# A two-layer encoder with streamed weights: one 512-column matmul in place of two of 256 in the weights-stationary products

## The chip, the cores and the metric

The kernel runs on one core of a Trainium2 chip. The metric is the device time of one execution in microseconds (us). The engines of the core work beside one another, each through its own list of instructions in a fixed order: TensorE (PE) multiplies matrices into PSUM, VectorE (DVE) and ScalarE (ACT) do elementwise work, GpSimd (POOL) does a little of it too, and SyncE (SP) issues most DMA transfers. An instruction waits at the head of its engine's list until the data and the buffers that it needs are there.

## The reference

The reference is an encoder trunk of two layers on 256 tokens of width 2048, all in float32. Cut to what is computed:

```python
for l in range(2):
    h = rmsnorm(x, attn_norm[l])
    qd, kd, vd, qn, kn, vn = split(h @ w_in[l])          # six blocks of 1024 columns
    o_diff = diff_attention(rope(qd), rope(kd), vd)      # 8 heads: softmax1 - lam * softmax2, then rmsnorm
    o_na   = rmsnorm(neighbourhood_attention(qn, kn, vn, rpb[l]))   # 8 heads, windows on a 4 x 64 grid
    x = x + concat(o_diff, o_na) @ w_out[l]
    u = relu(rmsnorm(x, mlp_norm[l]) @ w_mlp_in[l])      # 2048 -> 8192
    x = x + (u * u) @ w_mlp_out[l]                       # 8192 -> 2048
return rmsnorm(x, final_norm)
```

## The kernel before

**Numbers in two halves.** Every operand of a large product is split into a high half, rounded to the format that TensorE takes at full rate (fp32r), and a low half, what the rounding left. A product a·w is then three matmuls: a_hi·w_hi, a_lo·w_hi and a_hi·w_lo. Activations lie transposed in `hT` tiles, 16 of them (one for each 128 of the 2048 input columns), each with 256 high columns and, next to them in the same tile, 256 low columns.

**The weight stream.** The weights come in 384 slabs of 128 x 2048 float32 (1 MB). `next_slab` loads one into a `raw` buffer (three of them), ACT copies each half of 1024 columns to `whi` (line 130) and DVE subtracts to get `wlo` (line 131); there are four buffers of each.

**Two kinds of product.** `block_product` streams the weights through TensorE: 512 columns of weights move past 128 x 128 blocks of activations (lines 153 to 155), for two tiles of 128 tokens. `stationary_product` does it the other way round: a 128 x 128 block of weights is loaded into TensorE and the 256 tokens move past it, 16 blocks after one another into one PSUM tile `accu` of 128 x 256, three matmuls of 256 columns each (lines 180 to 182). It serves the queries and keys of the neighbourhood-attention heads (two products for each of 8 heads, in each of two layers, 32 in all) and the first product of the MLP (64 for each layer, 128 in all): 160 products of 16 steps, 2560 steps.

**What takes the results.** `accu` shares four PSUM banks with the `acc` tiles of `block_product` (tag "acc"). Queries go through `split_plain` (lines 276, 277), keys are first multiplied by `rb` (line 376); in the MLP ACT takes the Relu (`rl`, line 524) and DVE multiplies it by `accu` (line 526, u2), and `split` makes halves of that (lines 136, 137).

**The attention heads.** A differential head transposes its weights `wd` (line 296), ACT copies them out of PSUM (`wT`, line 303), PE multiplies by v (line 307), ACT squares the result with a running sum (`junk`, line 365), POOL makes a scale of it (lines 189, 191, 369), DVE applies it (`o`, line 315), PE transposes (line 318) and ACT and DVE split it into `mix` (lines 136, 137). A neighbourhood head transposes its weights `pr` (line 296), ACT and DVE split them (`half`, lines 276, 277), and PE multiplies by `vs` (lines 410 to 412). These PSUM results are called `tp` and share two banks. In SBUF, tag "o" is a ring of four buffers, in which a new tile waits until the one four before it is no longer read; `o`, `rl`, `u2` and a few smaller tiles are in it.

**The order.** The instructions of each engine are put in order at build time by the framework's scheduler, which simulates the program. So a change in the duration or number of instructions moves others too: PE's list mixes the long products with the small matmuls of the heads, and what stands between a small matmul and the next that needs its result is time in which ACT, DVE and POOL do their part.

Of the kernel before, what the change touches and what calls it, by code (L numbers as in the profile page):

```python
# [18 lines left out]
P = 128  # L19
# [16 lines left out]
NB = 512  # L36
NEG = -1.0e30
RUN = 5 * RPB_C + GRID_W
# Where a query of column 0 and an even row finds its last neighbour in a head's reversed table.
RPB_FIRST = RPB_HEAD - 1 - (10 * RPB_C + GRID_W - 1 + WIN_C - 1)  # L40
N_CHUNK = 4
F_PER_CHUNK = D_FF // P // N_CHUNK
SLABS = 48 + 16 + 64 + 64
# Column blocks of 512 of the input projection: q, k, v of the differential heads 0-3, then 4-7.
DIFF_BLOCKS = [0, 2, 4, 1, 3, 5]
NA_Q, NA_K, NA_V = 3 * HALF, 4 * HALF, 5 * HALF

# [1 line left out]
def body(ctx, tc, x, x_t, w, gains_in, gains_o, final_g, lam_in, rpb, ident_in, rope_in, mask_in, out):  # L49
# [5 lines left out]
    small = ctx.enter_context(tc.tile_pool(name="small", bufs=4))  # L55
    ps = ctx.enter_context(tc.tile_pool(name="ps", bufs=2, space=PSUM))

# [1 line left out]
    gin = const.tile([P, 2 * DEPTH, NK], F32, name="gin")  # L59
    nc.scalar.dma_start(gin, gains_in)  # L60
    ident = const.tile([P, P], F32, name="ident")
# [3 lines left out]
    xs = [const.tile([P, D], F32, name=f"x{t}") for t in range(NT)]  # L65

    def stream(dst, src):
        """A load on the queue of the weights, in the order of the program."""
        tc.keep_in_program_order(nc.sync.dma_start(dst, src))

    lam_sb = [None]

    def load_table(l):
        """The relative position biases of a layer, from where each query reads its windows."""
        table = act.tile([P, HEADS, RUN + 1], F32, name="table", tag="table", bufs=1)
        for rr in range(P // GRID_W):
            src = bass.AP(tensor=rpb.tensor,
                          offset=rpb.offset + l * HEADS * RPB_HEAD + RPB_FIRST + rr * RPB_C,
                          ap=[[1, GRID_W], [RPB_HEAD, HEADS], [1, RUN]])
            stream(table[rr * GRID_W:(rr + 1) * GRID_W, :, :RUN], src)  # L80
        return table
# [23 lines left out]
    ones = const.tile([P, P], F32, name="ones")  # L105
    nc.vector.memset(ones, 1.0)

# [1 line left out]
    slab_no = [0]  # L109
    x_rest = [None]  # L110

# [26 lines left out]
                                       op0=ALU.mult, op1=ALU.subtract)  # L138

    def block_product(n_k, operand, before=None, split_tail=0):  # L140
        """[256, 512] = sum over n_k blocks of 128 of operand(k)^T @ the next slabs. The last
        `split_tail` slabs are held together, so that one tile of tokens ends before the other."""
        acc = [ps.tile([P, NB], F32, name="acc", tag="acc", bufs=4) for _ in range(NT)]
        parts = []
        todo = []

        def one(k, t):
            hi, lo = parts[k // 2]
            c0 = (k % 2) * NB
            a = operand(k)  # L150
            wh, wl = hi[:, c0:c0 + NB], lo[:, c0:c0 + NB]
            ah, al = a[:, 0, t * P:(t + 1) * P], a[:, 1, t * P:(t + 1) * P]
            nc.tensor.matmul(acc[t], ah, wh, start=k == 0, stop=False)  # L153
            nc.tensor.matmul(acc[t], al, wh, start=False, stop=False)  # L154
            nc.tensor.matmul(acc[t], ah, wl, start=False, stop=k == n_k - 1)  # L155

        n_s = n_k // 4
        for s in range(n_s):
            if before is not None:
                before(s)  # L160
            parts += next_slab()
            todo += range(4 * s, 4 * s + 4)
            if s < n_s - split_tail:
                for k in todo:
                    for t in range(NT):
                        one(k, t)
                todo = []
        for t in range(NT):
            for k in todo:
                one(k, t)  # L170
        return acc

    def stationary_product(h_t):
        """[128, 256] = the next slab^T @ normed activations, transposed."""
        parts = next_slab()
        acc = ps.tile([P, S], F32, name="accu", tag="acc", bufs=4)
        for k in range(NK):
            hi, lo = parts[k // 8]
            wh, wl = hi[:, (k % 8) * P:(k % 8 + 1) * P], lo[:, (k % 8) * P:(k % 8 + 1) * P]
            nc.tensor.matmul(acc, wh, h_t[k][:, 0], start=k == 0, stop=False)  # L180
            nc.tensor.matmul(acc, wh, h_t[k][:, 1], start=False, stop=False)  # L181
            nc.tensor.matmul(acc, wl, h_t[k][:, 0], start=False, stop=k == NK - 1)  # L182
        return acc

# [1 line left out]
    def rms_scale(ss, n, width):  # L186
        """(ss / width + EPS) ** -0.5 on [128, n]."""
        v = small.tile([P, n], F32, name="v")
        nc.gpsimd.tensor_scalar(v, ss, 1.0 / width, EPS, op0=ALU.mult, op1=ALU.add)
        r = small.tile([P, n], F32, name="r")  # L190
        nc.gpsimd.tensor_tensor(r, v, mhalf[:, :n], op=ALU.pow)
        return r

    class Norm:
        """RMSNorm of x in pieces: the gain goes into the transposed halves, the scale of
        each token comes out of `scale()` and is applied to the products."""

        def __init__(self, gain):
            self.gain = gain
# [12 lines left out]
            self.h_t[k] = h  # L212

        def take(self, n):
            """Columns n*512... of x are final."""
            for t in range(NT):
                self.squares(n, t)
            for k in range(4 * n, 4 * n + 4):
                pt = ps.tile([P, S], F32, name="tp", tag="tp", bufs=2)
                for t in range(NT):  # L220
                    nc.tensor.transpose(pt[:, t * P:(t + 1) * P], xs[t][:, k * P:(k + 1) * P], ident)  # L221
                self.store(k, pt)
# [5 lines left out]
                self._r[t] = rms_scale(tot, 1, D)  # L228
            return self._r[t]

# [1 line left out]
    def to_sbuf_rope(acc, r, which):  # L232
        """Rotary position of q (which 0) or k (which 1), then transposed: [(m d), head, token]."""
        dst = [act.tile([P, 4, S], F32R, name="qkT", tag="A", bufs=12) for _ in range(2)]
        for t in range(NT):
            nat = work.tile([P, NB], F32, name="nat", tag="nat", bufs=3)
# [41 lines left out]
        return hi, lo  # L278

    def along_free(r):  # L280
        """[128, 256]: r of every token, in all partitions."""
        pb = ps.tile([P, S], F32, name="tp", tag="tp", bufs=2)
        for t in range(NT):
            diag = work.tile([P, P], F32, name="diag", tag="o", bufs=4)
            nc.vector.tensor_scalar(diag, ident, r[t], None, op0=ALU.mult)
            nc.tensor.matmul(pb[:, t * P:(t + 1) * P], ones, diag, start=True, stop=True)
        rb = work.tile([P, S], F32, name="rb", tag="rb", bufs=1)
        nc.scalar.activation(rb, pb, AF.Copy)
        return rb

    def transposed_weights(pr):
        """[128 queries, tile, 256 keys] -> [128 keys, tile, 256 queries] in PSUM."""
        pw = ps.tile([P, NT, S], F32, name="tp", tag="tp", bufs=2)
        for t in range(NT):
            for kt in range(NT):
                nc.tensor.transpose(pw[:, kt, t * P:(t + 1) * P], pr[:, t, kt * P:(kt + 1) * P], ident)  # L296
        return pw

    def weights_times_v(pr, v, j):
        """pr [128 q, tile, 256 keys] -> [128 q, tile, 128] in PSUM."""  # L300
        pw = transposed_weights(pr)
        wt = work.tile([P, NT, S], F32, name="wT", tag="wT", bufs=3)
        nc.scalar.activation(wt, pw, AF.Copy)
# [5 lines left out]
        return po  # L309

    def to_mix(po, scale, gain):
        """Scaled rows of po, transposed, with the gain, split."""
        o = work.tile([P, NT, HD], F32, name="o", tag="o", bufs=4)
        for t in range(NT):
            nc.vector.tensor_scalar(o[:, t, :], po[:, t, :], scale[:, t:t + 1], None, op0=ALU.mult)
        pt = ps.tile([P, S], F32, name="tp", tag="tp", bufs=2)
        for t in range(NT):
            nc.tensor.transpose(pt[:, t * P:(t + 1) * P], o[:, t, :], ident)
        return split_mix(pt, gain)
# [106 lines left out]
            else:  # L426
                nc.vector.scalar_tensor_tensor(sl, acc[t], scale[t], sl, op0=ALU.mult, op1=ALU.add)

# [1 line left out]
    norm = Norm(0)  # L430

    def prologue(s):
        """The transposed x comes in beside the first slabs, x itself and the tables behind them."""
        st = act.tile([P, 4, S], F32, name="xT", tag="A", bufs=12)

        def load(k0, k1):
# [10 lines left out]
    for l in range(DEPTH):  # L447
        if l == 0:
            first = [block_product(NK, norm.h_t.__getitem__, before=b) for b in (prologue, load_constants)]
            for t in range(NT):  # L450
                for n in range(4):
                    norm.squares(n, t)
            # lambda, and the sub-norm's gain times 1 - lambda_init
            lq = lam_sb[0].rearrange("p l (a b) d -> p l a b d", b=2)
            prod = work.tile([P, DEPTH, 2, QKD], F32, name="prod", tag="o", bufs=4)
            for i in range(DEPTH):
# [62 lines left out]
        for c in range(N_CHUNK):  # L519
            us = []  # L520
            for f in range(F_PER_CHUNK):
                acc = stationary_product(h_t)
                rl = work.tile([P, S], F32, name="rl", tag="o", bufs=4)
                nc.scalar.activation(rl, acc, AF.Relu)
                u2 = work.tile([P, S], F32, name="u2", tag="o", bufs=4)
                nc.vector.tensor_mul(u2, acc, rl)
                if f % 2 == 0:
                    pair = act.tile([P, 2, 2, S], F32R, name="u2T", tag="A", bufs=12)
                split(pair[:, f % 2, 0], pair[:, f % 2, 1], u2, 1.0)
# [13 lines left out]
                        nxt.take(n)  # L543
        norm = nxt

# [1 line left out]
    for t in range(NT):  # L547
        r = norm.scale(t)
        for n in (3, 0, 1, 2):
# [27 lines left out]
def _pack_weights(w_in, w_out, w_mlp_in, w_mlp_out):  # L577
    slabs = np.empty((DEPTH, SLABS, P, 2048), np.float32)

    def moving(a):  # L580
        """[K, N] -> [N / 512, K / 512, 128, 4 * 512]"""
        K, N = a.shape
        a = a.reshape(K // NB, 4, P, N // NB, NB).transpose(3, 0, 2, 1, 4)
        return a.reshape(N // NB, K // NB, P, 2048)

    def stationary(a):
        """[2048, N] -> [N / 128, 128, 16 * 128]"""
        return a.reshape(NK, P, -1, P).transpose(2, 1, 0, 3).reshape(-1, P, 2048)

    for l in range(DEPTH):  # L590
# [54 lines left out]
```

## Time and profile before

| | before |
|---|---|
| median of 3 runs | 2261.7 us (2261.6 to 2261.77) |
| span of the profiled execution | 2259.7 us |
| PE busy | 2244.5 us, 99% |
| DVE busy | 1296.5 us, 57% |
| ACT busy | 1063.4 us, 47% |
| POOL busy | 91.9 us, 4% |

The profiler took one execution. The whole of that execution was not timed apart from its span; the median of the runs is 2.0 us above the span, and that much is taken to lie around it. The shares are those of the span. "PE busy" counts an engine with work in its pipeline; how fast the pipeline goes is read from the distance of one matmul's start to the next one's.

### The profile page before, as it was taken

What the parts mean: (1) busy time and instruction counts of PE and PEld (TensorE: products, weight loads), DVE (VectorE), ACT (ScalarE), POOL (GpSimd) and SP (SyncE); (2) the same over time, 40 slices, a digit from 0 to 9 for tenths busy, and PEclk for the clock granted to TensorE, in tenths of its full rate; (3) what the DMA queues carried; (4) which work ended last, traced back from release to release, by engine and by line L of the source; (5) the groups of instructions that cost most, each with busy time, mean ns of one, the idle gap of its engine ahead of it and who ended that gap; (6) DMA issues with size and microseconds to landing.
All of it is one profiled execution on the core that took longest, in us unless ns stands there. A gap on an engine that the chain in (4) does not pass through costs nothing.

```text
span 2259.7 us, 33741 instructions
## 1 busy us (share of the span) xinstructions
PE 2244.5 (99%) x13904; PEld 2019.3 (89%) x13904; DVE 1296.5 (57%) x1615; ACT 1063.4 (47%) x1579; POOL 91.9 (4%) x136
## 2 busy tenths in 40 slices
PE   8999999999999999999999999999999999999998
PEld 7889998998998898899888899989989989988986
DVE  6656666655555555555566666665555555555554
ACT  6556454543444444344445564545434434444443
POOL 1111000000000000000010110000000000000000
PEclk9999999999999999999999999999999999999999
DMA  9453445555555545555654434455555555455553
GB/s 326 149 186 135 173 161 186 184 179 196 187 187 186 190 183 189 198 178 185 202 188 162 168 140 170 179 191 180 187 188 186 186 193 192 179 197 189 186 188 131
DMA packets 61306, 414.63 MB, mean 183 GB/s; under 512 B 7008, under 2 KB 9184, under 8 KB 11872
## 3 DMA queue, kind: packets, MB, share of 16 engines
q1 hardware_dynamic: 60720, 411.40, 50.8%
q8 instruction: 109, 1.79, 0.3%
q10 hardware_dynamic: 432, 1.08, 0.2%
q14 instruction: 45, 0.37, 0.0%
HBM read 410.35 MB, written 2.10 MB: 183 GB/s over the span
## 4 chain that ended last, share of the span: by engine, by line
PE 99%; DMA 0%; DVE 0%; ACT 0%; SPq 0%; issue 0%; POOL 0%; ACTq 0%; POOLq 0%
PE acc L155 18%; PE acc L153 18%; PE acc L154 18%; PE accu L180 14%; PE accu L182 14%; PE accu L181 14%; PE tp L307 1%; PE tp L296 1%; PE tp L221 0%; PE sc L343 0%; DMA raw<-in_w 0%; PE tp L257 0%; PE sc L345 0%; PE sc L344 0%; PE tp L412 0%; PE sc L387 0%
## 5 line engine op out<-in xcount | busy, mean ns | idle before, releaser
L131 DVE TENSOR_TENSOR wlo<-raw,whi 128x1024 fp32r<-128x1024 f32 (+1 forms) x770 | 945.7, 1229 | 848.0 <-ACT whi L130 841.4
L130 ACT ACTIVATE whi<-raw 128x1024 fp32r<-128x1024 f32 (+1 forms) x770 | 814.7, 1059 | 1055.5 <-PE acc L154 548.9
L181 PE MATMUL accu<-hT,whi 128*128 128x256 f32 x2560 | 726.0, 284 | 0.0
L182 PE MATMUL accu<-hT,wlo 128*128 128x256 f32 x2560 | 724.6, 283 | 0.0
L180 PE MATMUL accu<-hT,whi 128*128 128x256 f32 x2560 | 724.0, 283 | 0.0
L181 PEld LDWEIGHTS accu<-hT,whi 128*128 128x128 f32 x2560 | 491.5, 192 | 0.5
L180 PEld LDWEIGHTS accu<-hT,whi 128*128 128x128 f32 x2560 | 490.8, 192 | 0.8
L182 PEld LDWEIGHTS accu<-hT,wlo 128*128 128x128 f32 x2560 | 491.4, 192 | 0.0
L154 PE MATMUL acc<-whi,u2T 128*128 128x512 f32 x1024 | 399.2, 390 | 0.0
L153 PE MATMUL acc<-whi,u2T 128*128 128x512 f32 x1024 | 398.7, 389 | 0.0
L155 PE MATMUL acc<-wlo,u2T 128*128 128x512 f32 x1024 | 398.5, 389 | 0.0
L155 PEld LDWEIGHTS acc<-wlo,u2T 128*128 128x128 f32 x1024 | 192.3, 188 | 39.7
L153 PEld LDWEIGHTS acc<-whi,u2T 128*128 128x128 f32 x1024 | 192.3, 188 | 39.6
L154 PEld LDWEIGHTS acc<-whi,u2T 128*128 128x128 f32 x1024 | 192.3, 188 | 39.3
L153 PE MATMUL acc<-whi,hT 128*128 128x512 f32 x512 | 202.7, 396 | 6.0 <-ACT whi L130 6.0
L154 PE MATMUL acc<-whi,hT 128*128 128x512 f32 x512 | 203.0, 397 | 0.0
L155 PE MATMUL acc<-wlo,hT 128*128 128x512 f32 x512 | 199.4, 395 | 0.1
L153 PEld LDWEIGHTS acc<-whi,hT 128*128 128x128 f32 x512 | 96.9, 189 | 26.3 <-ACT whi L130 6.2
L155 PEld LDWEIGHTS acc<-wlo,hT 128*128 128x128 f32 x512 | 96.7, 189 | 20.3 <-DVE wlo L131 0.5
L154 PEld LDWEIGHTS acc<-whi,hT 128*128 128x128 f32 x512 | 96.9, 189 | 19.7
L154 PE MATMUL acc<-whi,mix 128*128 128x512 f32 x256 | 100.7, 393 | 0.0
L153 PE MATMUL acc<-whi,mix 128*128 128x512 f32 x256 | 100.7, 393 | 0.0
(117 smaller groups left out, 1331.9 us busy)
## 6 DMA issues: line engine op xcount, KB each, us to landing
raw<-in_w SPq DMA_DIRECT2D x383, 1024.0 KB, 4.8
x<-in_x SPq DMA_DIRECT2D x2, 1024.0 KB, 9.7
out<-xg SPq DMA_DIRECT2D x8, 256.0 KB, 3.1
table<-in_rpb SPq DMA_DIRECT2D x4, 438.0 KB, 11.5
xT<-in_x_t SPq DMA_DIRECT2D x3, 512.0 KB, 9.5
raw<-in_w SPq DMA_DIRECT2D x4, 256.0 KB, 5.4
gb<-in_final_g ACTq DMA_DIRECT2D x2, 512.0 KB, 5.7
xT<-in_x_t SPq DMA_DIRECT2D x2, 256.0 KB, 3.5
```

What stands on the lines that cost most here:

```text
L130: nc.scalar.activation(hi[:, c:c + step], r, AF.Copy)
L131: nc.vector.tensor_sub(lo[:, c:c + step], r, hi[:, c:c + step].bitcast(F32))
L153: nc.tensor.matmul(acc[t], ah, wh, start=k == 0, stop=False)
L154: nc.tensor.matmul(acc[t], al, wh, start=False, stop=False)
L155: nc.tensor.matmul(acc[t], ah, wl, start=False, stop=k == n_k - 1)
L180: nc.tensor.matmul(acc, wh, h_t[k][:, 0], start=k == 0, stop=False)
L181: nc.tensor.matmul(acc, wh, h_t[k][:, 1], start=False, stop=False)
L182: nc.tensor.matmul(acc, wl, h_t[k][:, 0], start=False, stop=k == NK - 1)
L296: nc.tensor.transpose(pw[:, kt, t * P:(t + 1) * P], pr[:, t, kt * P:(kt + 1) * P], ident)
L307: nc.tensor.matmul(po[:, t, :], wt[:, kt, t * P:(t + 1) * P], v[:, kt, j * HD:(j + 1) * HD], start=kt == 0, stop=kt == NT - 1)
```

## The change

`stationary_product` now issues two matmuls for each of its 16 steps instead of three. The first has 512 columns: the high and the low halves of the activations move past one load of the high weights, and their products go to the two halves of a PSUM tile that is now 512 columns wide. The second multiplies the low weights by the high activations and adds to the first half, as before. After the last step ACT copies the second half of the tile to SBUF (`low`, line 184) and DVE adds it to the first half (`whole`, line 186). What the function returns is therefore in SBUF, in the ring with tag "o". In the MLP the Relu on ACT goes, and DVE makes relu(u)·u in one instruction. Line numbers behind line 186 grow by four (line 296 becomes 300, 307 becomes 311, 318 becomes 322, 410 to 412 become 414 to 416). Comments are taken out, and the program gets a constant for a DMA scratch size.

```diff
     def stationary_product(h_t):
         parts = next_slab()
-        acc = ps.tile([P, S], F32, name="accu", tag="acc", bufs=4)
+        acc = ps.tile([P, NB], F32, name="accu", tag="acc", bufs=4)
         for k in range(NK):
             hi, lo = parts[k // 8]
             wh, wl = hi[:, (k % 8) * P:(k % 8 + 1) * P], lo[:, (k % 8) * P:(k % 8 + 1) * P]
-            nc.tensor.matmul(acc, wh, h_t[k][:, 0], start=k == 0, stop=False)
-            nc.tensor.matmul(acc, wh, h_t[k][:, 1], start=False, stop=False)
-            nc.tensor.matmul(acc, wl, h_t[k][:, 0], start=False, stop=k == NK - 1)
-        return acc
+            nc.tensor.matmul(acc, wh, h_t[k].rearrange("p a b -> p (a b)"), start=k == 0, stop=False)
+            nc.tensor.matmul(acc[:, :S], wl, h_t[k][:, 0], start=False, stop=k == NK - 1)
+        low = work.tile([P, S], F32, name="low", tag="low", bufs=2)
+        nc.scalar.activation(low, acc[:, S:], AF.Copy)
+        whole = work.tile([P, S], F32, name="whole", tag="o", bufs=4)
+        nc.vector.tensor_add(whole, acc[:, :S], low)
+        return whole
...
                 acc = stationary_product(h_t)
-                rl = work.tile([P, S], F32, name="rl", tag="o", bufs=4)
-                nc.scalar.activation(rl, acc, AF.Relu)
                 u2 = work.tile([P, S], F32, name="u2", tag="o", bufs=4)
-                nc.vector.tensor_mul(u2, acc, rl)
+                nc.vector.scalar_tensor_tensor(u2, acc, 0.0, acc, op0=ALU.max, op1=ALU.mult)
...
-    nc = bacc.Bacc("TRN2", target_bir_lowering=False, num_devices=1)
+    nc = bacc.Bacc("TRN2", target_bir_lowering=False, num_devices=1, dynamic_dma_scratch_size=4096)
```

The scheduler's order changes with it. Two places are shown. The first, **place A**, is the end of the differential heads, where the products of the neighbourhood heads begin. On PE before, in the first layer: `tp_1534` and `tp_1596` are the transposes of two heads' results `o`, `tp_1570` and `tp_1633` those of two heads' weights `wd`, `tp_1577` a head's product with v, and `accu_...` are weights-stationary products:

```order
L318 MATMUL tp_1534<-ident_75,o_1531 128x128
L181 MATMUL accu_1882<-hT_202,whi_1878 128x256
L318 MATMUL tp_1534<-ident_75,o_1531 128x128
L296 MATMUL tp_1570<-ident_75,wd_1567 128x128 x4
...
L307 MATMUL tp_1577<-v_1411,wT_1575 128x128 x4
...
L318 MATMUL tp_1596<-ident_75,o_1593 128x128
...
L296 MATMUL tp_1633<-ident_75,wd_1630 128x128 x4
```

The same place on PE now, with nothing left out:

```order
L182 MATMUL accu_1870<-hT_256,wlo_1867 128x256
L322 MATMUL tp_1534<-ident_75,o_1531 128x128 x2
L300 MATMUL tp_1570<-ident_75,wd_1567 128x128 x4
L311 MATMUL tp_1577<-v_1411,wT_1575 128x128 x4
L322 MATMUL tp_1596<-ident_75,o_1593 128x128 x2
L300 MATMUL tp_1633<-ident_75,wd_1630 128x128 x4
L181 MATMUL accu_1965<-hT_95,whi_1957 128x512
```

Before, 26 matmuls of the products stood between `tp_1570` and `tp_1577`, and 42 between that and `tp_1596`; now there are none. On ACT at place A before (`whi` are weight halves, `half` and `kr` belong to the neighbourhood heads, `junk` is the square, `vs` the split values):

```order
L136 ACTIVATE mix_1474<-tp_1534,gsub_82 128x256
L303 ACTIVATE wT_1575<-tp_1570 128x512
L130 ACTIVATE whi_2048<-raw_2042 128x1024
L276 ACTIVATE half_1933<-kr_1931 128x256
L365 ACTIVATE junk_1583,sso_1582<-tp_1577,rs_1563 128x128
L365 ACTIVATE junk_1585,sso_1582<-tp_1577,rs_1563 128x128
L130 ACTIVATE whi_2152<-raw_2150 128x1024
L136 ACTIVATE mix_1599<-tp_1596,gsub_82 128x256
L136 ACTIVATE vs_1803<-acc_1665,r_473 128x512
```

And now; DVE's part of `vs` (line 137) follows ACT's:

```order
L130 ACTIVATE whi_2012<-raw_2006 128x1024
L184 ACTIVATE low_1903<-accu_1870 128x256
L136 ACTIVATE mix_1474<-tp_1534,gsub_82 128x256
L307 ACTIVATE wT_1575<-tp_1570 128x512
L369 ACTIVATE junk_1583,sso_1582<-tp_1577,rs_1563 128x128
L369 ACTIVATE junk_1585,sso_1582<-tp_1577,rs_1563 128x128
L136 ACTIVATE mix_1599<-tp_1596,gsub_82 128x256
L136 ACTIVATE vs_1803<-acc_1665,r_473 128x512
```

The two weight halves and the `half` that stood between these steps stand elsewhere; a weight half (`whi_2012`) and `low_1903` now stand ahead of `mix_1474`. The product behind place A, `accu_1965`, takes the PSUM bank of `acc_1665`; DVE now has the last reader of `accu_1819` (`whole_1854`) behind `vs` in its list.

The second, **place B**, is in the neighbourhood heads' second group of four. On PE before, in the first layer (`tp_2787` the transposed weights of a head, `tp_2796` its product with `vs`):

```order
L180 MATMUL accu_2990<-hT_95,whi_2982 128x256
L296 MATMUL tp_2787<-ident_75,pr_2779 128x128 x4
L181 MATMUL accu_2990<-hT_95,whi_2982 128x256
...
L182 MATMUL accu_2990<-hT_202,wlo_2987 128x256
L410 MATMUL tp_2796<-half_2792,vs_2631 128x256
L411 MATMUL tp_2796<-half_2792,vs_2632 128x256
```

The corresponding head's place on PE now, with nothing left out:

```order
L182 MATMUL accu_2897<-hT_256,wlo_2894 128x256
L300 MATMUL tp_2667<-ident_75,pr_2659 128x128 x4
L414 MATMUL tp_2676<-half_2672,vs_2535 128x256
L415 MATMUL tp_2676<-half_2672,vs_2536 128x256
L416 MATMUL tp_2676<-half_2673,vs_2535 128x256
```

Before, 31 matmuls stood between the transposes and the products that need ACT's and DVE's halves of them; now there are none. The next head (**place C**, `tp_2815` behind `accu_3045`) has the same order, and the second layer repeats all three places. At B a weight half (`whi_3041`, of `next_slab`) stands ahead of `half_2672` on ACT, and its low half (`wlo_3042`) ahead of `half_2673` on DVE; `whi_3041` takes the buffer of the last half that `accu_2897` reads.

## Rows read from the trace of the kernel before

**Rows 1.** The page's parts 1 and 4.
```profile
PE 2244.5 (99%) x13904; PEld 2019.3 (89%) x13904; DVE 1296.5 (57%) x1615; ACT 1063.4 (47%) x1579; POOL 91.9 (4%) x136
...
PE 99%; DMA 0%; DVE 0%; ACT 0%; SPq 0%; issue 0%; POOL 0%; ACTq 0%; POOLq 0%
```
**Rows 2.** PE timeline, a weights-stationary product: start, duration (us), engine, line, operands.
```profile
449.81 0.28 PE L180 MATMUL accu<-hT,whi 128*128 128x256 f32 x1
...
453.05 0.28 PE L180 MATMUL accu<-hT,whi 128*128 128x256 f32 x1
```
**Rows 3.** PE timeline, a product with moving weights, 512 columns.
```profile
699.79 0.39 PE L155 MATMUL acc<-wlo,u2T 128*128 128x512 f32 x1
...
711.81 0.39 PE L154 MATMUL acc<-whi,u2T 128*128 128x512 f32 x1
```
**Rows 4.** Windows: length, busy PE, PEld, DVE, ACT, POOL, clock, DMA, GB/s.
```profile
425.00:485.00 60.00, 60.00 (x503) 60.00 (x502) 35.16 (x46) 29.82 (x46) 0.00 (x0) 1.00 0.52 182
```
**Rows 5.** Lines by form: count, then busy us, mean ns, idle before.
```profile
L524 ACT ACTIVATE rl<-accu 128x256 f32<-128x256 f32 x128 | 46.9, 367 | 0.0
L526 DVE TENSOR_TENSOR u<-accu,rl 128x256 f32<-128x256 f32 x128 | 53.4, 417 | 0.0
L137 DVE SCALAR_TENSOR_TENSOR vs<-acc,r,vs 128x512 fp32r<-128x512 f32 x8 | 5.8, 748 | 0.4
L136 ACT ACTIVATE vs<-acc,r 128x512 fp32r<-128x512 f32 x8 | 5.3, 689 | 0.0
```
**Rows 6.** PE timeline of the last differential heads, 181 to 202 us.
```profile
186.13 0.38 PE L318 MATMUL tp<-ident,o 128*128 128x128 f32 x2
...
189.56 1.05 PE L307 MATMUL tp<-v,wT 128*128 128x128 f32 x8
190.37 0.36 PE L182 MATMUL accu<-hT,wlo 128*128 128x256 f32 x1
...
200.34 1.05 PE L307 MATMUL tp<-v,wT 128*128 128x128 f32 x8
```
**Rows 7.** ACT timeline of the heads, 196 to 203 us.
```profile
196.05 1.06 ACT L130 ACTIVATE whi<-raw 128x1024 fp32r<-128x1024 f32 x1 [1.55 <-PE accu L181]
197.01 0.46 ACT L136 ACTIVATE mix<-tp,gsub 128x256 fp32r<-128x256 f32 x1
197.42 0.60 ACT L303 ACTIVATE wT<-tp 128x512 f32<-128x512 f32 x1
...
201.51 0.37 ACT L365 ACTIVATE junk<-tp,rs 128x128 f32<-128x128 f32 x1 [0.57 <-PE tp L307]
...
202.27 0.19 ACT L365 ACTIVATION_READ_ACCUMULATOR junk<-tp,rs 128x1 f32 x1
```
**Rows 8.** POOL and DVE timelines of the heads.
```profile
203.59 0.19 POOL L369 TENSOR_TENSOR comb<-r,rs 128x2 f32<-128x2 f32 x1
...
182.97 0.61 DVE L315 TENSOR_SCALAR o<-tp,comb 128x128 f32<-128x128 f32 x2 [0.51 <-POOL comb L369]
```
**Rows 9.** ACT and DVE timelines of a neighbourhood head, 226 to 231 us.
```profile
227.77 0.60 ACT L276 ACTIVATE half<-tp 128x512 fp32r<-128x512 f32 x1 [1.78 <-PE tp L296]
...
228.71 0.68 DVE L277 TENSOR_TENSOR half<-tp,half 128x512 fp32r<-128x512 f32 x1
229.40 1.23 DVE L131 TENSOR_TENSOR wlo<-raw,whi 128x1024 fp32r<-128x1024 f32 x1
```
**Rows 10.** PE's start and end, and windows at the end.
```profile
5.96 0.80 PE L153 MATMUL acc<-whi,hT 128*128 128x512 f32 x1 [5.96 <-ACT whi L130]
...
11.24 0.47 PE L153 MATMUL acc<-whi,hT 128*128 128x512 f32 x1
...
2250.16 0.39 PE L155 MATMUL acc<-wlo,u2T 128*128 128x512 f32 x1
2253.60:2253.80 0.20, 0.00 (x0) 0.00 (x0) 0.20 (x2) 0.20 (x1) 0.00 (x0) 1.00 1.17 338
2254.00:2254.20 0.20, 0.00 (x0) 0.00 (x0) 0.20 (x1) 0.20 (x2) 0.00 (x0) 0.50 0.67 236
```

## The prediction

> **What bounds the kernel now.** I read the page's part 1 and the chain of waits first, then the PE timeline, then windows and groups by line, and last the timelines of the heads. In part 1 the reader is to see PE busy for 99% of the span, with DVE at 57% and ACT at 47%, and in the chain PE with 99% of the path [rows 1]. So nothing but PE's list counts: a matmul made shorter is a gain, a wait of PE's is a loss, and work on another engine counts only where PE waits for it. The PE timeline gives the rate at which the list runs. In a weights-stationary product 27 steps take 453.05 − 449.81 = 3.24 us, 0.1200 us for each 256-column matmul [rows 2]. Where 512 columns move, 53 steps take 711.81 − 699.79 = 12.02 us, 0.2268 us each [rows 3]. Twice the columns take 1.89 times as long, not twice: a line through the two has 0.0132 us for each matmul and 0.000417 us for each column.
>
> **The merged matmul.** A step of 128 weights took three narrow matmuls, 3 x 0.1200 = 0.3600 us. It will take a wide and a narrow one, 0.2268 + 0.1200 = 0.3468 us, if the wide one with fixed weights runs at the pitch of the wide one with moving weights. The saving is 0.0132 us a step, over 2560 steps 33.8 us. The trace shows no wide matmul in this kind of product. From one side it could take as long as two narrow ones (0.2400, no saving), from the other no more than its columns (512 x 0.000417 = 0.2134, 68.1 us saved). I take 0.2268, the row with the same shape and type, and keep both ends.
>
> The Trainium skill (TensorE: Matmul & The Clock Gate, section "Back-to-back issue gap") gives an isolated matmul a fixed 2.5 ns beside its columns, and says that a stream of loads and matmuls is paced by both. By 2.5 ns the estimate would be 2560 x 0.0025 = 6.4 us saved; the trace disagrees, with 13.2 ns between two widths that both run in streams with a load for each [rows 2, 3].
>
> **What is added on ACT and DVE.** Each of the 160 products gets a copy on ACT (nearest row: the Relu of the same tile, 367 ns) and an addition on DVE (nearest: 417 ns) [rows 5]. In the MLP the copy takes the Relu's place, and DVE's product becomes one instruction of two operations, about the 417 ns that it took, so there only the addition is new: 0.42 us in a product of 16 x 0.3468 = 5.55 us. While PE was busy for 60.00 us in the MLP, DVE had 35.16 and ACT 29.82 us of work [rows 4]: DVE goes to some 70%. Four PSUM banks let a product's result wait for two products without stopping PE. I cost this at nothing; the cover is the next product, and if all of it stood open it would be 160 x 0.42 = 67 us. The DMA was busy for 0.52 of this stretch at 182 GB/s [rows 4] and has room for 4% more speed. The scratch constant adds no instruction.
>
> **What the new order adds.** At place A five groups of small matmuls stand behind one another on PE, each needing what ACT, POOL or DVE make of an earlier one, and no product between. Before, 26 and 42 narrow matmuls covered the two longest steps, 3.1 and 5.0 us at 0.1200. I follow the chain from the end of the product `accu_1870`, time 0. A hop between engines is 0.12 us: ACT starts at 201.51 on what PE ended at 200.34 + 1.05 [rows 6, 7]. `whi_2012`, whose buffer comes free at time 0, starts at 0.12 and lets the next ACT work start 0.96 later (196.05 to 197.01), at 1.08 [rows 7]. Then `low` 0.37 [rows 5], `mix` 0.41 and `wT` 0.60 [rows 7]: 2.46. Hop and product with v, 0.12 + 1.05 [rows 6]: 3.63. Hop and the two squares, 0.12 + 0.95 (201.51 to 202.46) [rows 7]: 4.70. POOL's scale, from 202.46 to 203.78, 1.32 [rows 7, 8]: 6.02. DVE's `o`, 0.65 with its 0.04 of waiting [rows 8]: 6.67. Hop and transposes, 0.50 [rows 6]: 7.17. `mix` 0.46 [rows 7]: 7.63. Then `vs` on ACT 0.69 and on DVE 0.75 [rows 5]: 9.07, and a hop: PE can start `accu_1965`, which takes the bank that `vs` empties, at 9.2. Of this 20 small matmuls at 0.10 each (eight of them from 189.56 to 190.37, 0.81) [rows 6] were PE's work before as well, 2.0. Wait: 7.2 us. Behind `accu_1965` on PE is everything else, so nothing hides it. From below it is 0, if PE comes so late that the other engines are ahead; from above it is the whole chain, 9.2.
>
> At place B the products with `vs` stand directly behind the transposes whose halves they need. `whi_3041` starts at 0.12, ACT's `half` at 1.08; DVE has `wlo_3042` from 1.22 to 2.45 (1.23), then its `half` to 3.13 (0.68) [rows 7, 9]. A hop and the last four products at 0.12 end at 3.73; PE's own ten matmuls are 1.1. Wait: 2.6 us, where 31 narrow matmuls, 3.7 us, were the cover before. Place C has the same order: 2.6.
>
> All three stand in both layers: 2 x (7.2 + 2.6 + 2.6) = 24.8 us.
>
> **The sum.** The profiled span is 2259.7; 2.0 us around it make the median, 2261.7, and nothing of the change touches the start or the tail behind PE's last matmul. 2259.7 − 33.8 + 24.8 = 2250.7, and 2252.7 with the 2.0: I predict 2253, 9 us faster. Three quarters of the saving goes into waits.
>
> **Rivals.**
>
> *The clock falls at place A.* PE's granted clock is 1.00 up to the last matmul, which starts at 2250.16, and still at 2253.60; from 2254.00 it is 0.50, the lower of the two levels, after PE had done nothing [rows 10]. So a stop of the end's kind is answered by a fall. At the start of the run 12 wide matmuls take 11.24 − 5.96 = 5.28 us where 12 x 0.2268 = 2.72 would do [rows 10]: 2.6 us for one return from the lower clock. For: at A PE has 9.2 us with 2.0 of work. Against: that work is spread over the wait, the longest piece with none, from the product with v to the transposes, is 6.79 − 3.63 = 3.2 us, and the stop at the end is 9 us long. Two falls: 2252.7 + 5.2 = 2257.9, within 0.2%, which is 4.5 us and about what a measurement of this kernel can tell from no change.
>
> *The clock falls at all six waits.* The same mechanism, at B and C too: 6 x 2.6 = 15.6, 2268.3. It decides from the fourth fall on (4 x 2.6 = 10.4 against a gain of 9.0). Against: PE stops for less than 3 us at B and C. The Trainium skill (TensorE: Matmul & The Clock Gate, "HAM oscillation — how this bites in real kernels") tells of a kernel whose stops between bursts brought the lower clock back every time; no stop in the middle of this trace tests it, since PE has none of any length.
>
> *The waits are mostly hidden.* The order was planned with durations of its own; where PE comes later to a place than I think, or ACT earlier with `whi`, less is open. If half of the 24.8 is open the time is 2240.3, if none 2227.9. For: B and C hang on whether ACT gets at a weight half before the `half`, and a head start of 1 us takes 1 us off each. Against: the buffers of `whi` come free only with the product before, and PE's list has no product there to fill in.
>
> *The merge saves nothing.* A wide matmul takes 0.2400: 2261.7 + 24.8 = 2286.5, slower. For: the fixed part could belong to the change of weights and not to the matmul. Against: the moving-weights products change weights at each matmul too and run at 0.2268 [rows 3]. With the skill's 2.5 ns it would be an estimate of 2280.
>
> **Chances.** Forecast 0.52; fall at A 0.20; waits mostly hidden 0.14; fall at all six 0.09; nothing saved 0.05. The forecast and the hidden waits are faster (0.66), and of the falls at A, which end beside the bound, two fifths: 0.74. The other three fifths are within 0.2%, with a little from the falls at some of the six: 0.14. Slower 0.12. The range leaves out the slower cases and the end of the hidden waits: 2238 (some 60% of the waits hidden, 2252.7 − 14.9) to 2261 (falls at A, and 3 of the 8.4 us by which the whole chains, 9.2 and twice 3.7 in each layer, are above the waits). The likeliest case's own range is 2247 to 2256.
>
> **What would show it.** The PE timeline of an MLP product: a wide matmul followed 0.227 later by the narrow one, 0.120 to the next. PE's idle time: some 7 us at two places ahead of a wide matmul whose releaser is DVE's `vs`, 2 to 3 us at four ahead of the products with `vs`, and next to none in the MLP. The granted clock: 1.00 through the middle slices. Wrong would be a wide pitch at 0.24, a DVE or ACT releaser ahead of products in the MLP, or matmuls at twice their pitch behind A.

## The result, and the profile after

The changed kernel takes 2276.55 us (median of 4 runs, 2276.06 to 2277.01), the kernel before 2261.65 in the same session: ratio 1.0066, 95% interval 1.0052 to 1.008. It is 14.9 us slower where 9 us faster was forecast, and outside the range.

The page's first and fourth parts of the changed kernel, which answer to [rows 1]:

```profile
PE 2238.0 (98%) x11344; PEld 1887.9 (83%) x11344; DVE 1363.4 (60%) x1775; ACT 1073.4 (47%) x1611; POOL 103.2 (5%) x136
...
PE 97%; ACT 1%; DVE 1%; DMA 1%; POOL 0%; issue 0%; ACTq 0%; POOLq 0%
```

PE is still what ends last, but no longer alone: ACT and DVE have a share of the chain. And 2560 matmuls fewer have taken only 6.5 us off PE's busy time, though 33.8 were forecast. Where PE stood still is the table of its waits (line, what released it: us in total, times, longest):

```profile
PE acc L153 <- ACT whi L130: 8.3, 4, 6.5
PE tp L322 <- DVE o L319: 5.7, 2, 2.8
PE tp L414 <- ACT half L280: 4.0, 4, 1.1
PE tp L416 <- DVE half L281: 3.5, 4, 0.9
PE tp L311 <- ACT wT L307: 3.0, 2, 1.5
PE accu L181 <- DVE vs L137: 2.4, 2, 1.3
PE accu L182 <- DVE wlo L131: 0.3, 2, 0.2
```

The first row is the start of the run (6.5 and 0.8) and two waits of 0.5; the last, 0.3 us, lies in the MLP. The five between are the three places of the prediction, in both layers, with the releasers that it named. Place A on PE in the first layer:

```profile
199.44 0.28 PE L182 MATMUL accu<-hT,wlo 128*128 128x256 f32 x1
...
199.77 0.60 PE L300 MATMUL tp<-ident,wd 128*128 128x128 f32 x4
201.87 1.16 PE L311 MATMUL tp<-v,wT 128*128 128x128 f32 x8 [1.50 <-ACT wT L307]
205.87 0.73 PE L322 MATMUL tp<-ident,o 128*128 128x128 f32 x2 [2.84 <-DVE o L319]
...
208.53 0.80 PE L181 MATMUL accu<-hT,whi 128*128 128x512 f32 x1 [1.08 <-DVE vs L137]
...
212.38 0.40 PE L181 MATMUL accu<-hT,whi 128*128 128x512 f32 x1
```

From the last matmul of `accu_1870` at 199.44 to `accu_1965` at 208.53 are 9.1 us with 2.1 of PE's own work: a wait of 7.0, against 7.2 forecast. (The table has 5.4 of it, since it counts a matmul as busy for its whole time in the pipeline.) Place B in the same layer is told the same way:

```profile
308.61 0.28 PE L182 MATMUL accu<-hT,wlo 128*128 128x256 f32 x1
...
310.46 0.39 PE L414 MATMUL tp<-half,vs 128*128 128x256 f32 x1 [0.87 <-ACT half L280]
...
311.84 0.39 PE L416 MATMUL tp<-half,vs 128*128 128x256 f32 x1 [0.87 <-DVE half L281]
...
312.42 0.39 PE L181 MATMUL accu<-hT,whi 128*128 128x512 f32 x1
```

From 308.61 to 312.42 are 3.8 us with 1.2 of PE's own work, a wait of 2.6; place C has the same.

Then look at what follows place A: the six steps of 128 weights from 208.53 to 212.38 take 3.85 us where 6 x 0.3467 = 2.08 would do. The windows say why (length; busy time of PE, PEld, DVE, ACT, POOL; clock; DMA share; GB/s):

```profile
205.40:212.10 6.70, 5.16 (x17) 4.20 (x18) 2.50 (x5) 2.12 (x4) 0.03 (x1) 0.50 0.11 44
212.20:310.00 97.80, 97.32 (x554) 84.52 (x553) 65.99 (x100) 52.30 (x92) 13.76 (x11) 1.00 0.46 162
328.30:331.60 3.30, 3.30 (x9) 2.58 (x8) 1.58 (x4) 2.02 (x6) 0.74 (x1) 0.50 0.74 300
1441.00:1444.30 3.30, 3.30 (x13) 2.91 (x13) 1.78 (x6) 2.02 (x6) 0.74 (x1) 0.50 0.86 315
```

The granted clock falls to its lower level, 1.2 GHz, at place A, and again at places B and C: five times in the execution (A in both layers, C in both, B in the second; not B in the first, which has the same two stops of 0.87), where before it was never below 1.00 between the run's first microseconds and its last matmul [rows 10].

The third reading is the rate in the MLP, which answers to [rows 2]. Two stretches of the same line of the program, in the first and in the second of the four chunks:

```profile
455.24 0.40 PE L181 MATMUL accu<-hT,whi 128*128 128x512 f32 x1
...
460.78 0.40 PE L181 MATMUL accu<-hT,whi 128*128 128x512 f32 x1
...
619.93 0.40 PE L181 MATMUL accu<-hT,whi 128*128 128x512 f32 x1
...
625.94 0.40 PE L181 MATMUL accu<-hT,whi 128*128 128x512 f32 x1
```

Sixteen steps in the first take 5.54 us, 0.3463 each, as forecast. Seventeen in the second take 6.01, 0.3535. Over whole products the two rates are 0.3467 and 0.3533. In each layer the last ten products of the first chunk go at the faster rate and all 48 of the other three at the slower, without a wait in either.

Matching the n-th matmul that takes low weights in both traces gives the account of the 14.9 us. The start is 1.0 us later. From the end of the differential heads to the MLP the first layer loses 13.7 and the second 15.7; each MLP gains 7.8. Of the losses, waits are 7.0 and 6.8 at A, and 2.6 at B and 2.6 at C in each layer, 24.2 together. The lower clock costs 1.8 at A in the first layer and 2.4 in the second (eight steps from 1336.93 to 1342.11 take 5.18 us where 2.77 would do), and 1.6 at each of the three other falls, 9.0 together. `whi` ahead of line 153 makes 0.5 twice. That is 24.2 + 9.0 + 1.0 = 34.2 against a measured 29.4, so the merge is taken to have saved the rest there, 4.8; with the 15.6 of the two MLPs, which are measured, it saved 20.4.

### The profile page after: what moved, and what is told of

The parts are those of the page before. It is cut to its first block, busy times and chain, and to the rows that moved or that the text cites. A ratio compares the mean times of both kernels' runs of the same rounds, so it can differ in the third digit from the quotient of the medians.

```text
span 2274.6 us, 28845 instructions
## 1 busy us (share of the span) xinstructions
PE 2238.0 (98%) x11344; PEld 1887.9 (83%) x11344; DVE 1363.4 (60%) x1775; ACT 1073.4 (47%) x1611; POOL 103.2 (5%) x136
## 4 chain that ended last, share of the span: by engine, by line
PE 97%; ACT 1%; DVE 1%; DMA 1%; POOL 0%; issue 0%; ACTq 0%; POOLq 0%
PE accu L181 26%; PE acc L154 18%; PE acc L153 18%; PE acc L155 18%; PE accu L182 13%; PE tp L311 1%; ACT whi L130 1%; PE tp L225 0%; PE tp L300 0%; DMA raw<-in_w 0%; PE sc L347 0%; DVE wlo L131 0%; PE tp L261 0%; PE tp L416 0%; PE sc L349 0%; PE sc L348 0%
## 5 line engine op out<-in xcount | busy, mean ns | idle before, releaser
L181 PE MATMUL accu<-hT,whi 128*128 128x512 f32 x2560 | 909.3, 399 | 2.4 <-DVE vs L137 2.4
L181 PEld LDWEIGHTS accu<-hT,whi 128*128 128x128 f32 x2560 | 483.2, 189 | 118.5 <-DVE vs L137 3.2
L182 PEld LDWEIGHTS accu<-hT,wlo 128*128 128x128 f32 x2560 | 485.7, 190 | 1.8 <-DVE wlo L131 1.0
L155 PE MATMUL acc<-wlo,mix 128*128 128x512 f32 x256 | 100.7, 396 | 0.0
L186 DVE TENSOR_TENSOR whole<-accu,low 128x256 f32<-128x256 f32 x160 | 65.6, 418 | 0.0
```

The source lines that it names most:

```text
L181: nc.tensor.matmul(acc, wh, h_t[k].rearrange("p a b -> p (a b)"), start=k == 0, stop=False)
L182: nc.tensor.matmul(acc[:, :S], wl, h_t[k][:, 0], start=False, stop=k == NK - 1)
L186: nc.vector.tensor_add(whole, acc[:, :S], low)
```

## The experiments

**The ring.** A possible reason for the new order is that `whole` shares its buffers with the heads' tiles, so that its sum stands behind them on DVE and keeps a PSUM bank. The trace of the changed kernel bears this out: ACT's copies of two products are done at 195.4 and 201.0, but both sums stand behind the next `o` on DVE, so that two of the four banks are held until 217.72 and later:

```profile
200.60 0.37 ACT L184 ACTIVATE low<-accu 128x256 f32<-128x256 f32 x1
...
217.19 0.61 DVE L319 TENSOR_SCALAR o<-tp,comb 128x128 f32<-128x128 f32 x2 [1.73 <-POOL comb L373]
217.72 0.74 DVE L186 TENSOR_TENSOR whole<-accu,low 128x256 f32<-128x256 f32 x2
```

One edit gives `whole` a ring of its own:

```diff
-        whole = work.tile([P, S], F32, name="whole", tag="o", bufs=4)
+        whole = work.tile([P, S], F32, name="whole", tag="whole", bufs=4)
```

> The changed kernel with one edit: the sum `whole` gets four buffers of its own in place of the ring "o" that it shares with the heads' tiles. Theory 1 (the ring holds the PSUM banks, so the scheduler's order leaves the six places open, and the clock falls at five of them): the waits of 24 us and some 9 us of matmuls at the lower clock go, 2276.5 - 33 = 2243; with the step of 128 weights at 0.3467 throughout instead of partly 0.3533 it is 2230. PE has no wait over 1 us between its first and last matmul and the clock stays at 1.00. Theory 2 (the waits come with the extra pass over ACT and DVE itself, wherever the sum lies): waits stay, above 2270.

Measured: 2243.87 us (2242.62 to 2244.79, 4 runs), ratio to before 0.9922 (0.9908 to 0.9937). All of PE's waits, the 6.1 ahead of its first matmul among them:

```profile
PE acc L153 <- ACT whi L130: 7.4, 2, 6.1
PE accu L182 <- DVE wlo L131: 0.3, 2, 0.2
```

And the same place A, with the clock of the whole stretch below it:

```profile
199.30 0.60 PE L300 MATMUL tp<-ident,wd 128*128 128x128 f32 x4
199.66 0.48 PE L181 MATMUL accu<-hT,whi 128*128 128x512 f32 x1
...
204.68 1.05 PE L311 MATMUL tp<-v,wT 128*128 128x128 f32 x8
...
195.00:430.00 235.00, 234.83 (x1261) 201.15 (x1260) 154.57 (x229) 124.60 (x214) 20.91 (x30) 1.00 0.47 166
```

Products stand again between the transposes of `wd` and the product with v, 5 us of them, and DVE makes the sum of the product that ended at 199.1 from 201.40. Waits and falls are gone with one tag; theory 2 is refuted. The two executions that were profiled (2276.65 and 2242.62) are 34.0 apart: 24.2 of waits, 9.0 of clock, 1.0 of `whi` and 0.5 of the start, less 0.9 by which the attention stages gain less from the merge here, which makes 33.8. The MLPs gain the same 15.6, at the same two rates. The edit gives the program four more buffers and not only another tag; a larger ring that is still shared was not tried.

**The merge undone.** With the same buffers, the three narrow matmuls of before:

```diff
-            nc.tensor.matmul(acc, wh, h_t[k].rearrange("p a b -> p (a b)"), start=k == 0, stop=False)
+            nc.tensor.matmul(acc[:, :S], wh, h_t[k][:, 0], start=k == 0, stop=False)
+            nc.tensor.matmul(acc[:, :S], wh, h_t[k][:, 1], start=False, stop=False)
...
-        nc.scalar.activation(low, acc[:, S:], AF.Copy)
+        nc.scalar.activation(low, acc[:, :S], AF.Copy, scale=0.0)
```

> `whole` in four buffers of its own, and the merge undone: three narrow matmuls a step into the first half of the PSUM tile, as before the change; the copy on ACT then takes the first half times zero, so that both passes stay but add nothing. It measures what the passes over ACT and DVE cost without merge and without the shared ring. If they are hidden, 2262 (within 3 us of before); if they cost what theory 2 of the first run says, above 2270. Its difference to the kernel with the merge and the same buffers is what the merge alone saves: 33.8 at one rhythm, 17 at the other.

Measured: 2261.73 us (10 runs), ratio 1.0001 (0.9992 to 1.0011). The added passes over ACT and DVE cost nothing, nor does the scratch constant, which this version has too. The merge alone saves 2261.73 − 2243.87 = 17.9 us, 0.0070 a step: about half of the forecast, the slower rate nearly throughout.

**Groups of eight.** In the changed kernel with its shared ring, the widths no longer take turns:

```diff
-        for k in range(NK):
...
+        for half in range(2):
+            hi, lo = parts[half]
+            for k in range(8 * half, 8 * half + 8):
+                wh = hi[:, (k % 8) * P:(k % 8 + 1) * P]
+                nc.tensor.matmul(acc, wh, h_t[k].rearrange("p a b -> p (a b)"), start=k == 0, stop=False)
+            for k in range(8 * half, 8 * half + 8):
+                wl = lo[:, (k % 8) * P:(k % 8 + 1) * P]
+                nc.tensor.matmul(acc[:, :S], wl, h_t[k][:, 0], start=False, stop=k == NK - 1)
```

> The changed kernel with one edit: in each half slab the eight wide matmuls come first and the eight narrow ones after them, instead of taking turns. The ring stays shared. Theory 1 (taking turns of two widths runs in one of two rhythms, 0.3467 or 0.3533 us a step, while a stream of one width runs at 0.2267 or 0.1200): every MLP step at 0.3467, 12 to 14 us faster than the changed kernel, 2263; the waits at A, B and C stay where the order keeps them. Rival (the 0.3533 comes from the memory the operands lie in or from what else is read then): no change of the step, 2276.

Measured: 2258.42 us (10 runs), ratio 0.9988 (0.9979 to 0.9998): 18.1 faster than the changed kernel, more than expected. In the MLP groups of eight follow one another evenly:

```profile
613.77 2.00 PE L182 MATMUL accu<-hT,whi 128*128 128x512 f32 x8
...
622.15 2.00 PE L182 MATMUL accu<-hT,whi 128*128 128x512 f32 x8
```

Three groups of each width, 24 steps, take 8.38 us, 0.3492 a step. Over 2560 steps that saves 27.6 us against 20.4. A, B and C are still there, with the same releasers (5.7 for `o`, 2.4 for `vs`), but the waits for `half` fell from 7.5 to 4.7 and those for `wT` from 3.0 to 1.6, and the clock fell only at A, twice, three falls fewer. So the slow rate hangs on the order of the widths; the other 11 us of the gain are waits and clock, which the regrouping moved as well.

**Both edits.**

> Both edits: `whole` in four buffers of its own, and eight wide matmuls ahead of eight narrow ones. If the two causes are independent: all of the saving, 33.8 us, and none of the waits: 2261.7 - 33.8 + 1 = 2229. If either theory is wrong: 2243 (waits alone gone) or 2263 (rhythm alone gone).

Measured: 2235.74 us (2234.56 to 2237.27), ratio 0.9887 (0.9872 to 0.9902). The two causes are separate, but 2229 was not reached: a step is 0.3492, not 0.3467, and 2261.7 less 2560 x 0.0108 is 2234.1. The profiled execution (2236.87) also has a fall of the clock at 16.9 us, behind a wait of 1.4 for `whi`, and is 2.0 later from there on. The profiled executions of the version with sixteen and of `own_entry` below have such a fall too, and the other versions have none there; differences of 2 us between these versions are therefore not read from the times.

**Where the widths change.** Groups of sixteen, and pairs (2 in place of 16), both with `whole` in its own buffers:

```diff
-        for k in range(NK):
...
+        for g in range(0, NK, 16):
+            for k in range(g, g + 16):
+                wh = parts[k // 8][0][:, (k % 8) * P:(k % 8 + 1) * P]
...
+            for k in range(g, g + 16):
+                wl = parts[k // 8][1][:, (k % 8) * P:(k % 8 + 1) * P]
...
```

> `whole` in four buffers of its own, and all sixteen wide matmuls of a product ahead of its sixteen narrow ones. Theory (each change between the two widths costs some 0.02 us until the stream settles): half the changes of the version with groups of eight, 160 x 0.023 = 3.6 us less than its 2235.7, so 2232. Rival (the wide matmul with fixed weights simply takes 0.2306, wherever it stands): no difference, 2236.

> `whole` in four buffers of its own, and two wide matmuls ahead of two narrow ones, in turns. By the theory that changes of width cost, it lies between taking turns (2243.9) and groups of eight (2235.7), with a change every two matmuls nearer to the former: 2240 to 2244. By the rival (only the pitch of the wide matmul counts) it is 2236 to 2238.

Measured: 2234.16 us (ratio 0.9877, 0.9862 to 0.9892) and 2233.98 (ratio 0.9879, 0.9865 to 0.9894). A product of the version with sixteen, on PE:

```profile
620.53 3.82 PE L181 MATMUL accu<-hT,whi 128*128 128x512 f32 x16
624.19 2.08 PE L184 MATMUL accu<-hT,wlo 128*128 128x256 f32 x16
626.10 0.40 PE L181 MATMUL accu<-hT,whi 128*128 128x512 f32 x1
```

The time lies between the 2232 and the 2236 that the two theories gave, so it is the intervals that decide. Sixteen wide matmuls take 3.66 us, 0.2288 each; singly, the first five stand 0.233, 0.236, 0.228, 0.233 and 0.231 apart and the rest 0.2267. So a change to the wide form does cost some 0.02 us before the stream settles, as expected. But pairs, with eight times as many changes, refute it as the whole account: they came out below both of the ranges that were expected. Three periods of that version:

```profile
619.77 0.63 PE L181 MATMUL accu<-hT,whi 128*128 128x512 f32 x2
620.24 0.39 PE L184 MATMUL accu<-hT,wlo 128*128 128x256 f32 x2
...
621.86 0.63 PE L181 MATMUL accu<-hT,whi 128*128 128x512 f32 x2
```

Six steps take 2.09 us, 0.3483 each: most of what the wide matmul pays behind a change (0.233 in place of 0.2267), the narrow one gets back (0.115 on average in place of 0.120).

**The start of the stream.** That left a rhythm: a stream that takes turns can go at 0.3467 or 0.3533, and the first chunk, whose first products have transposes among them, found the faster one. Now `whole` has its own buffers, only the first product of each MLP chunk is in pairs (`lead`), and the others take turns as in the change:

```diff
-                acc = stationary_product(h_t)
+                acc = stationary_product(h_t, lead=f == 0)
```

> `whole` in four buffers of its own; wide and narrow matmuls take turns as in the change, but the first of the sixteen products of each MLP chunk has them in pairs. Theory (a stream that takes turns keeps the rhythm with which it starts): a product in pairs ahead sets the faster one, and the fifteen products behind it run at 0.347 a step instead of 0.3533 in the six chunks that were slow: 6 x 15 x 16 x 0.0067 = 9.6 us less than 2243.9, so 2234 to 2236. Rival (something else in those chunks, not the start, sets it): they return to 0.3533 and only the six products in pairs gain, 0.6 us: 2243.

Measured: 2233.58 us (2232.96 to 2235.96, 4 runs), ratio 0.9874 (0.9858 to 0.9891). In the second chunk, which was slow, now behind the product in pairs:

```profile
617.63 0.39 PE L182 MATMUL accu<-hT,whi 128*128 128x512 f32 x1
...
624.90 0.40 PE L182 MATMUL accu<-hT,whi 128*128 128x512 f32 x1
```

Twenty-one steps in 7.27 us, 0.3462. All six chunks that had been slow now go at 0.3467 behind their product in pairs. So the same instructions on the same data go at either rate, and what came ahead can set it.

The order ahead does not settle it alone. In the first chunk of this version PE's list is the same in both layers, and in both it waits 0.32 us for `wlo` in the fourth product (at 431.91 and at 1541.10). Behind that wait the two layers part:

```profile
440.59 0.40 PE L182 MATMUL accu<-hT,whi 128*128 128x512 f32 x1
...
445.19 0.40 PE L182 MATMUL accu<-hT,whi 128*128 128x512 f32 x1
...
1549.66 0.40 PE L182 MATMUL accu<-hT,whi 128*128 128x512 f32 x1
...
1554.52 0.40 PE L182 MATMUL accu<-hT,whi 128*128 128x512 f32 x1
```

Thirteen steps in the first layer take 4.60 us, 0.354 each, and fourteen in the second 4.86, 0.347. With the product in pairs ahead, the first layer's first chunk went from the faster rate to the slower. What inside PE sets the rhythm and keeps it stays open.

**The clock.** The changed kernel, with work for PE in the wait for `o` at place A (`fill` is 12 for the third head of the second group, else 0):

```diff
+        for _ in range(fill):
+            nc.tensor.matmul(pt[:, :P], ones, ident, start=True, stop=True)
```

> The changed kernel with twelve matmuls of constants (128 x 128, float32, some 2.4 us by the 0.2 us each of the product with v) put into the bank of `tp_1596` ahead of its transposes, at place A of both layers; their result is overwritten. They run inside the 2.8 us for which PE waits for `o`, and PE's order is otherwise that of the changed kernel. Theory (the clock falls because PE does nothing): the waits for data stay, but the clock no longer falls at A: about 2.1 us less at each of two places, 2272, with the falls behind B and C as they were. Rival (the clock falls for the low work of the whole stage, or at a fixed point of the program): the falls at A stay and the time is 2276 to 2277.

Measured: 2271.6 us (2269.92 to 2271.99, 5 runs), ratio to before 1.0042 (1.0028 to 1.0056), 4.95 below the changed kernel. Place A, and three windows of that run (A in the first and in the second layer, B in the first):

```profile
202.90 2.84 PE L322 MATMUL tp<-ident,ones 128*128 128x128 f32 x24
205.89 0.58 PE L324 MATMUL tp<-ident,o 128*128 128x128 f32 x2 [0.15 <-DVE o L319]
...
208.41 0.50 PE L181 MATMUL accu<-hT,whi 128*128 128x512 f32 x1 [1.49 <-DVE vs L137]
...
205.40:212.10 6.70, 5.06 (x31) 4.04 (x30) 2.50 (x5) 2.79 (x5) 0.05 (x1) 1.00 0.12 49
1329.80:1337.00 7.20, 5.56 (x43) 4.87 (x43) 2.59 (x6) 3.03 (x8) 1.08 (x3) 1.00 0.40 148
310.40:313.70 3.30, 3.30 (x13) 2.92 (x12) 1.82 (x5) 2.02 (x6) 0.73 (x1) 0.50 0.82 305
```

`accu_1965` starts at 208.41 instead of 208.53: the chain of data is as long as it was. But the clock stays at 1.00 through A, in both layers. So the fall there comes from PE's idleness and not from the place. Three falls are left, at C in both layers and at B in the first. That last one (310.4) was not there in the changed kernel, and the one at B in the second layer is gone. So 1.8 and 2.4 us at A and 1.6 at B are saved and 1.6 is new: 4.2 of the 4.95 us; the rest was not separated.

## Why the prediction was wrong, point by point

Two steps failed: the saving of the merged matmul was sized too large, and the fall of the clock, which the same waits brought with them, was put at nothing in the forecast.

- **What bounds the kernel, and the passes on ACT and DVE:** right. PE's waits in the MLP are 0.3 us in all, and the two passes cost nothing (2261.73 with them and without the merge).
- **What the new order adds:** right. 24.2 us of waits against 24.8, at the three places, with the releasers and the chain named; A is 7.0 and 6.8 against 7.2, B and C 2.6 each as forecast. Only the sign was put loosely: the 7 us do not stand ahead of one wide matmul, but in three pieces ahead of lines 311, 322 and 181.
- **The merged matmul:** this term was mis-sized, 20.4 us instead of 33.8. The pitch of a stream of one width [rows 3] was taken for a stream in which two widths take turns. That stream runs at 0.3467 or at 0.3533 a step, and three quarters of the MLP's products got the slower. The value lay between the two ends that were named (0 and 68.1), but the range was built on 33.8 alone. Even the faster rate meets the forecast's 0.3468 partly by luck: its wide matmul takes 0.232 and its narrow one 0.115, not 0.2268 and 0.1200 (the slower one has 0.237 and 0.117). The trace before could not show it, since no stream there changes its width at every step.
- **The clock:** the forecast had no fall; it gave 0.20 to falls at A and 0.09 to falls everywhere. There were five of six. The argument against, that PE works in between, failed: at A the work between the stops did not keep the clock up, and at B and C it fell just behind the second of two stops of 0.9 to 1.1 us, 0.5 us of work apart. The comparison with a stop of 9 us at the end was a misreading too: by [rows 10] the clock there fell between 2253.8 and 2254.0, less than 3.5 us after PE's last work ended at 2250.55, hardly more than the 3.2 us forecast for the longest piece at A. The price was put somewhat too high, 2.6 a fall against 1.6 to 2.4. 9.0 us in all.
- **The sum:** 13.4 from the merge, 9.0 from the clock, 2.0 from the start and the two waits of 0.5, less 0.6 on the waits: 23.8 of the 23.9 between 2252.7 and 2276.55. It closes because the merge's part in the attention stages (4.8) is what the other terms leave over; the experiment with the merge undone puts the merge at 17.9. The smaller saving and the falls stood in the prediction as separate cases; they came together, and the range allowed for neither the falls at B and C nor a smaller saving.
- **The rival "waits mostly hidden":** did not come. Without the shared ring PE has no such waits, but there the order is another.

## What to carry to other kernels

Give a result that must leave PSUM a buffer of its own: put into a ring that slower work shares, it holds the bank, and here the scheduler's order left PE standing at six places. When PE is the bound, count a stop twice, for its length and for the clock behind it (here 9.0 us on 24.2). And take the rate of a stream from a stream with the same pattern: groups or pairs of equal matmuls gave 0.348 to 0.349 a step in the MLP, single turns gave 0.347 or 0.353 by what came ahead, and not always by the order alone. The change with its own buffers and the widths in pairs takes 2233.98 us, 1.2% below the kernel before.

## What the runs showed of the hardware

A stream of alternating 512- and 256-column matmuls ran at one of two rates, 0.3467 and 0.3533 us a pair, with no wait in the profile at either. A single product in another order ahead of it moved the 15 products behind from the slower to the faster in six chunks of six; in the first chunk, behind a wait of 0.32 us, the same list of matmuls went at the slower rate in one layer and at the faster in the other. In groups of sixteen, the first wide matmuls behind a change from 256 to 512 columns stand 0.233 and 0.236 us apart and settle at 0.2267 after five; behind the other change the first narrow one takes 0.113 in place of 0.120. And the clock fell at place A with no single stop of PE longer than 2.84 us; filling that stop alone with matmuls kept it up.
